# Chaining the two heads' weights-times-values products of a dense pair, key block by key block

## Chip, cores and metric

One NeuronCore of a Trainium2 chip runs the whole kernel. The metric is the device time of one execution in microseconds; the median of three runs of the kernel before is 1922.91 us (1922.61 to 1922.99). The granted TensorE clock was 0.997 of the full clock over the profiled execution.

## The reference, cut to what matters

The reference is a network of five mixing layers and one feed-forward layer over 512 tokens of width 1024. Three kinds of layer use dense causal softmax attention, which is where the change lies: the NSA layer (8 heads; its selected-block branch and its window branch both cover all earlier keys at this length), the MLA layer (twice, 16 heads) and the FOX layer (16 heads, with a forget term in the scores). The sliding-window layer has a code of its own. The dense part is

```
s = q @ k.T * scale            # 512 x 512 a head, keys after the query masked out
p = softmax(s)
o = p @ v                      # head width 64
```

## The kernel before, in words

All data is float32. Projections, scores and the output products are made of two- or three-term splits (`fp32r` tiles named `h` and `l`; lines 273 to 275, 309 and 310). The transposes of the softmax weights (line 335) and their products with the values (line 342) are plain float32 matmuls, and each of these float32 matmuls shows as two records of TensorE in the trace.

Heads are worked two at a time, a pair. For each head `dense_head` goes over the four blocks of 128 queries: scores into a PSUM tile `s`, mask and row maximum on VectorE (line 322), exponential on ScalarE (line 325), scaling by the reciprocal of the sum on VectorE (line 329), into an SBUF tile `sp`. Then it goes over the four blocks of 128 keys, j = 0 to 3: the 4 - j blocks of weights that see these keys are transposed on TensorE into a PSUM tile `t` (two buffers), and ScalarE copies the result into the SBUF tile `pt` (line 336, which calls the helper whose instruction is on line 205). So block j of `pt` has 512, 384, 256 or 128 columns.

`dense_values` then multiplies, for each key block j and each of the two heads i, the values of that block (128 keys x 64 channels, the stationary operand) with block j of the head's `pt`, and accumulates in one PSUM tile `o` (one buffer): head 0 in partitions 0 to 63, head 1 in partitions 64 to 127. That is 8 matmuls for each pair and branch. The FOX layer has 8 pairs, each MLA layer 8, and the NSA branch has 4 pairs with two branches each, 32 pairs in all. `gated` (line 950), or a copy, takes the pair's result out of `o`.

The program is written with a tile framework. Its scheduler orders the instructions of each engine once, when the kernel is built: a list scheduler with a timeline simulation that takes, for each engine, the earliest instruction in program order that is ready at that moment. It places the semaphores. So the order on an engine is not that of the source: the projections of the next heads, of gates (`gates`, `gate_tile`) and, in NSA, of `fill_gate` and `fill_up` are later in the program and are set into gaps. At run time each engine works through its fixed order.

In the three callers the two heads' `dense_head` come first and then `dense_values` (lines 790 to 792, 1059 to 1061, 1268 to 1270):

```
pt.append(self.dense_head(P, scores))
...
po = self.pso()
self.dense_values(po, pt, lambda jj, hh: ...)
```

The tile `pt` has two buffers in these stages, `sp` two (three in NSA).

Of the kernel before, what the change touches and what calls it, by code (L numbers as in the profile page):

```python
# [13 lines left out]
AF = mybir.ActivationFunctionType  # L14
# [6 lines left out]
NB = 4  # L21
# [28 lines left out]
TOFF = [0, 512, 896, 1152]  # L50
# [77 lines left out]
class Net:  # L128
# [73 lines left out]
            self.vcopy(out, in_, scale)  # L202

    def acopy(self, out, in_, scale=None):
        self.nc.scalar.activation(out, in_, AF.Copy, scale=1.0 if scale is None else scale)  # L205

    def vcopy(self, out, in_, scale=None):
        if scale is None:
# [103 lines left out]
    def dense_head(self, P, scores, gate=None, bufs=None):  # L312

        nc = self.nc
        sp = P.tile([128, 1280], F32, name="sp", bufs=bufs)
        mx, nm, sm, rc = (self.sm(NB, n) for n in ("mx", "nm", "sum", "rc"))
        for b in range(NB):
            n, g = (b + 1) * 128, slice(b, b + 1)
            v = sp[:, POFF[b]:POFF[b] + n]
            ps = self.pss()[:, 0:n]  # L320
            scores(ps, slice(b * 128, n), slice(0, n))
            nc.vector.tensor_tensor_reduce(  # L322
                out=v, in0=ps, in1=self.causal[:, S - n:S], scale=1.0, scalar=LOWEST, op0=ALU.add, op1=ALU.max, accum_out=mx[:, g])
            nc.vector.tensor_scalar(nm[:, g], mx[:, g], -1.0, None, ALU.mult)  # L324
            nc.scalar.activation(v, v, AF.Exp, bias=nm[:, g], accum_out=sm[:, g])  # L325
            nc.vector.reciprocal(rc[:, g], sm[:, g])
            if gate is not None:
                nc.vector.tensor_tensor(out=rc[:, g], in0=rc[:, g], in1=gate[:, g], op=ALU.mult)
            nc.vector.tensor_scalar(v, v, rc[:, g], None, ALU.mult)  # L329
        pt = P.tile([128, 1280], F32, name="pt")  # L330
        for j in range(NB):
            ps = self.pst()
            n = (NB - j) * 128
            for b in range(j, NB):
                nc.tensor.transpose(ps[:, (b - j) * 128:(b - j + 1) * 128], sp[:, POFF[b] + j * 128:POFF[b] + j * 128 + 128], self.ident)  # L335
            self.acopy(pt[:, TOFF[j]:TOFF[j] + n], ps[:, 0:n])
        return pt

    def dense_values(self, po, pts, value, first=True, last=True):
        for j in range(NB):  # L340
            for i, pt in enumerate(pts):
                self.nc.tensor.matmul(  # L342
                    po[64 * i:64 * i + 64, j * 128:S], lhsT=value(j, i), rhs=pt[:, TOFF[j]:TOFF[j] + (NB - j) * 128],
                    start=first and j == 0, stop=last and j == NB - 1, skip_group_check=not (first and last))


    def to_feat(self, src, b, scale=None, pool=None):
# [965 lines left out]
```

## Time and profile before

| what | value |
|---|---|
| median of three runs | 1922.91 us |
| the profiled execution | 1921.38 us |
| its span, first to last instruction | 1919.6 us |
| TensorE busy (matmul) | 1880.0 us, 98% |
| VectorE busy | 1153.4 us, 60% |
| ScalarE busy | 878.2 us, 46% |
| GpSimd busy | 156.4 us, 8% |
| mean load on 16 DMA engines | 77 GB/s |

The profile is of one execution. Busy time is the time in which an engine has at least one instruction open. The records of TensorE overlap, since a matmul is let in before the one ahead has drained, and their ends are modelled; the distance from one start to the next tells how long one matmul holds TensorE.

### The profile page before, as it was taken

The numbers are of one execution on the slowest core, as the hardware profiler recorded it, in microseconds if no ns is written. First come the engines' busy times: TensorE is split into PE (matmuls) and PEld (weight loads), VectorE is DVE, ScalarE is ACT, GpSimd is POOL, SyncE is SP. The second block draws the span as 40 slices with busy tenths as digits, with TensorE's granted clock in tenths as the row PEclk, the third lists the DMA queues.
The fourth block names the chain that finished last, engine by engine and source line by source line (L and its number), as shares of the span: only waits on it lengthen the run. The fifth ranks groups of instructions, "written<-read, shape, count | busy, mean of one in ns | idle before, by whom it ended". The sixth has DMA issues, their size and how long they took to land.

```text
span 1919.6 us, 26637 instructions
## 1 busy us (share of the span) xinstructions
PE 1880.0 (98%) x9843; PEld 1496.4 (78%) x9843; DVE 1153.4 (60%) x2954; ACT 878.2 (46%) x1970; POOL 156.4 (8%) x213
## 2 busy tenths in 40 slices
PE   8999899999999999999999999999999999999997
PEld 7777677678888888889777788877887777987775
DVE  5554486754533343256878675577765665787765
ACT  4543245642322132135666434563555563466651
POOL 2221200000000000001000011251000000200001
PEclk9999999999999999999999999999999999999999
DMA  7222041042422243133221133212422231231111
GB/s 212 78 55 67 4 133 50 17 133 87 122 88 82 75 129 99 60 95 96 56 62 55 56 100 91 67 53 60 110 66 55 67 96 49 76 88 49 58 45 44
DMA packets 200781, 148.09 MB, mean 77 GB/s; under 512 B 8797, under 2 KB 178570, under 8 KB 200650
## 3 DMA queue, kind: packets, MB, share of 16 engines
q1 hardware_dynamic: 198858, 140.97, 25.4%
q0 software_dynamic: 1792, 5.42, 0.9%
q8 instruction: 77, 1.26, 0.3%
q14 instruction: 54, 0.44, 0.1%
HBM read 144.27 MB, written 2.10 MB: 76 GB/s over the span
## 4 chain that ended last, share of the span: by engine, by line
PE 84%; DVE 2%; issue 1%; ACT 1%; POOL 0%; DMA 0%; POOLq 0%; DVEq 0%; ACTq 0%
PE pj L273 22%; PE pj L275 21%; PE pj L274 21%; PE o L342 6%; PE t L335 4%; PE s L273 1%; PE s L309 1%; PE s L274 1%; PE s L275 1%; PE s L310 1%; PE t L358 1%; PE t L1166 1%; PE s L1265 1%; PE s L1266 1%; PE o L1121 1%
## 5 line engine op out<-in xcount | busy, mean ns | idle before, releaser
L214 ACT ACTIVATE wh<-wr 128x1024 fp32r<-128x1024 f32 (+9 forms) x390 | 281.3, 749 | 459.5 <-PE pj L274 272.5
L215 DVE TENSOR_TENSOR wl<-wr,wh 128x1024 fp32r<-128x1024 f32 (+9 forms) x390 | 321.7, 847 | 229.2 <-ACT wh L214 226.6
L273 PE MATMUL pj<-Ah,wh 128*128 128x512 f32 (+1 forms) x1120 | 434.8, 389 | 1.3 <-DVE k4l L215 0.8
L274 PE MATMUL pj<-Al,wh 128*128 128x512 f32 (+1 forms) x1120 | 433.5, 387 | 0.0
L275 PE MATMUL pj<-Ah,wl 128*128 128x512 f32 (+1 forms) x1120 | 433.5, 388 | 0.0
L273 PEld LDWEIGHTS pj<-Ah,wh 128*128 128x128 f32 x1120 | 210.6, 188 | 47.6 <-issue 3.1
L275 PEld LDWEIGHTS pj<-Ah,wl 128*128 128x128 f32 x1120 | 210.8, 188 | 45.2 <-issue 2.2
L274 PEld LDWEIGHTS pj<-Al,wh 128*128 128x128 f32 x1120 | 210.8, 188 | 43.3 <-issue 1.6
L273 PE MATMUL pj<-wh,Ah 128*128 128x512 f32 (+5 forms) x640 | 218.5, 342 | 3.8 <-ACT Ah L214 3.8
L274 PE MATMUL pj<-wl,Ah 128*128 128x512 f32 (+5 forms) x640 | 216.5, 339 | 0.0
L275 PE MATMUL pj<-wh,Al 128*128 128x512 f32 (+5 forms) x640 | 214.6, 340 | 0.5 <-DVE Al L215 0.4
L325 ACT ACTIVATE sp<-sp,nm 128x128 f32<-128x128 f32 (+3 forms) x256 | 142.7, 558 | 95.6 <-DVE nm L324 93.6
L322 DVE CUSTOM_DVE_ANT_0 sp<-s,c_causal 128x128 f32<-128x128 f32 (+3 forms) x256 | 121.9, 487 | 90.7 <-PE s L275 38.7
L205 ACT ACTIVATE pt<-t 128x512 f32<-128x512 f32 (+3 forms) x288 | 119.5, 445 | 122.9 <-PE t L335 99.3
L273 PEld LDWEIGHTS pj<-wh,Ah 128*128 128x128 f32 x640 | 121.5, 190 | 19.3 <-ACT Ah L214 5.7
L275 PEld LDWEIGHTS pj<-wh,Al 128*128 128x128 f32 x640 | 121.0, 190 | 15.4 <-issue 2.4
L274 PEld LDWEIGHTS pj<-wl,Ah 128*128 128x128 f32 x640 | 121.6, 190 | 11.6 <-issue 1.1
L335 PE MATMUL t<-ident,sp 128*128 128x128 f32 x640 | 111.7, 279 | 2.4 <-ACT pt L205 2.3
L335 PEld LDWEIGHTS t<-ident,sp 128*128 128x128 f32 x640 | 76.6, 140 | 47.2 <-ACT pt L205 16.8
L329 DVE TENSOR_SCALAR sp<-sp,rc 128x128 f32<-128x128 f32 (+3 forms) x256 | 96.7, 383 | 4.5
L342 PE MATMUL o<-pt,vt 128*64 128x512 f32 (+3 forms) x384 | 92.2, 452 | 0.0
L274 PE MATMUL pj<-wl,hdh 128*128 128x512 f32 x176 | 68.3, 390 | 0.0
(417 smaller groups left out, 2853.7 us busy)
## 6 DMA issues: line engine op xcount, KB each, us to landing
wr<-in_w_in_dram SPq DMA_DIRECT2D x34, 512.0 KB, 3.8
wr<-in_fox_w_in_dram SPq DMA_DIRECT2D x30, 512.0 KB, 4.2
wr<-in_w_ffn_gate_dram SPq DMA_DIRECT2D x22, 512.0 KB, 3.9
wr<-in_w_ffn_up_dram SPq DMA_DIRECT2D x22, 512.0 KB, 4.1
wr<-in_w_ffn_down_dram SPq DMA_DIRECT2D x20, 512.0 KB, 3.6
wr<-in_swa_w_in_dram SPq DMA_DIRECT2D x20, 512.0 KB, 4.4
wr<-in_mla_w_in_dram SPq DMA_DIRECT2D x16, 512.0 KB, 4.4
wr<-in_mla_w_out_dram SPq DMA_DIRECT2D x16, 512.0 KB, 3.8
```

What stands on the lines that cost most here:

```text
L205: self.nc.scalar.activation(out, in_, AF.Copy, scale=1.0 if scale is None else scale)
L214: self.nc.scalar.activation(h, src, AF.Copy)
L215: self.nc.vector.tensor_tensor(out=l, in0=src, in1=h.bitcast(F32), op=ALU.subtract)
L273: self.nc.tensor.matmul(ps, lhsT=ah, rhs=bh, start=i == 0, stop=False)
L274: self.nc.tensor.matmul(ps, lhsT=ah, rhs=bl, start=False, stop=False)
L275: self.nc.tensor.matmul(ps, lhsT=al, rhs=bh, start=False, stop=i == n - 1)
L309: self.nc.tensor.matmul(ps, lhsT=q, rhs=kh, start=True, stop=False)
L322: nc.vector.tensor_tensor_reduce(out=v, in0=ps, in1=self.causal[:, S - n:S], scale=1.0, scalar=LOWEST, op0=ALU.add, op1=ALU.max, accum_out ...
L325: nc.scalar.activation(v, v, AF.Exp, bias=nm[:, g], accum_out=sm[:, g])
L329: nc.vector.tensor_scalar(v, v, rc[:, g], None, ALU.mult)
L335: nc.tensor.transpose(ps[:, (b - j) * 128:(b - j + 1) * 128], sp[:, POFF[b] + j * 128:POFF[b] + j * 128 + 128], self.ident)
L342: self.nc.tensor.matmul(po[64 * i:64 * i + 64, j * 128:S], lhsT=value(j, i), rhs=pt[:, TOFF[j]:TOFF[j] + (NB - j) * 128], start=first and ...
```

## The change

`acopy` returns its instruction, `dense_head` returns its `pt` together with the last of its four copies, and a new helper `after` records a dependency between two instructions. In `dense_values` the heads are taken in the order 1, 0 for each key block. The first of the eight matmuls gets a real dependency (with a wait) on the last copy of both heads; each further matmul is only told to stand behind the one before it on the same engine, which needs no semaphore.

```diff
     def acopy(self, out, in_, scale=None):
-        self.nc.scalar.activation(out, in_, AF.Copy, scale=1.0 if scale is None else scale)
+        return self.nc.scalar.activation(out, in_, AF.Copy, scale=1.0 if scale is None else scale)
...
-            self.acopy(pt[:, TOFF[j]:TOFF[j] + n], ps[:, 0:n])
-        return pt
+            turned = self.acopy(pt[:, TOFF[j]:TOFF[j] + n], ps[:, 0:n])
+        return pt, turned.ins
+
+    def after(self, later, earlier, how=mybir.DependencyClass.NoSync):
+        self.tc.add_manual_dep(later, earlier.name, mybir.DependencyInfo(how, mybir.DependencyReason.DATA), reason="order")
 
     def dense_values(self, po, pts, value, first=True, last=True):
+
+        prev = None
         for j in range(NB):
-            for i, pt in enumerate(pts):
-                self.nc.tensor.matmul(
+            for i in (1, 0):
+                pt, turned = pts[i]
+                mm = self.nc.tensor.matmul(
                     po[64 * i:64 * i + 64, j * 128:S], lhsT=value(j, i), rhs=pt[:, TOFF[j]:TOFF[j] + (NB - j) * 128],
-                    start=first and j == 0, stop=last and j == NB - 1, skip_group_check=not (first and last))
+                    start=first and j == 0, stop=last and j == NB - 1, skip_group_check=not (first and last)).ins
+                if prev is None:
+                    for _, t in pts:
+                        self.after(mm, t, mybir.DependencyClass.Sync)
+                else:
+                    self.after(mm, prev)
+                prev = mm
```

## Rows read from the trace of the kernel before

**Rows 1.** The page: span, and TensorE's busy time, share and instructions.
```profile
span 1919.6 us, 26637 instructions
...
PE 1880.0 (98%) x9843; PEld 1496.4 (78%) x9843; DVE 1153.4 (60%) x2954; ACT 878.2 (46%) x1970; POOL 156.4 (8%) x213
```
**Rows 2.** Windows of a stage: from:to, length, busy us (count) of each engine, clock, DMA.
```profile
915.00:1085.00 170.00, 169.62 (x879) 125.42 (x878) 128.76 (x432) 104.33 (x280) 1.14 (x2) 1.00 0.19 59
...
380.00:390.00 10.00, 10.00 (x56) 6.79 (x56) 8.41 (x49) 7.30 (x23) 0.00 (x0) 1.00 0.17 53
```
**Rows 3.** Line 342 alone: its window; its first and last visit in TensorE's timeline.
```profile
0.00:1920.00 1920.00, 123.35 (x512) 38.26 (x512) 1.00 0.27 77
...
286.32 1.07 PE L342 MATMUL o<-pt,X 128*64 128x512 f32 x2
...
1878.69 1.51 PE L342 MATMUL o<-pt,vt 128*64 128x384 f32 x10
```
**Rows 4.** TensorE's timeline, one MLA pair: start us, busy us, line, operation, count.
```profile
933.51 0.49 PE L335 MATMUL t<-ident,sp 128*128 128x128 f32 x3
933.93 1.07 PE L342 MATMUL o<-pt,vt 128*64 128x512 f32 x2
934.93 0.33 PE L273 MATMUL s<-k4h,qh 128*128 128x128 f32 x1
...
941.91 1.07 PE L342 MATMUL o<-pt,vt 128*64 128x512 f32 x4
...
943.30 0.86 PE L342 MATMUL o<-pt,vt 128*64 128x384 f32 x4
...
946.73 0.65 PE L342 MATMUL o<-pt,vt 128*64 128x256 f32 x4
...
947.78 0.43 PE L342 MATMUL o<-pt,vt 128*64 128x128 f32 x2
```
**Rows 5.** TensorE's timeline, a later pair: longer visits, seven transposes, the score after.
```profile
966.59 1.72 PE L342 MATMUL o<-pt,vt 128*64 128x512 f32 x8
...
971.22 0.86 PE L342 MATMUL o<-pt,vt 128*64 128x256 f32 x6
972.02 0.98 PE L335 MATMUL t<-ident,sp 128*128 128x128 f32 x7
972.76 0.42 PE L273 MATMUL s<-k4h,qh 128*128 128x384 f32 x1
```
**Rows 6.** TensorE's timeline, sliding-window layer: first record of a visit, the instruction after it.
```profile
1204.10 0.54 PE L1121 MATMUL o<-pt,vt 128*64 128x128 f32 x5
...
1205.77 0.33 PE L309 MATMUL s<-k0h,q 128*128 128x128 f32 x1
```
**Rows 7.** Timelines: two pairs' last copies on ScalarE, the second's last visit on TensorE.
```profile
966.59 0.55 ACT L205 ACTIVATE pt<-t 128x256 f32<-128x256 f32 x2 [1.03 <-PE t L335]
...
1818.77 0.28 ACT L205 ACTIVATE pt<-t 128x128 f32<-128x128 f32 x1 [0.46 <-PE t L335]
...
1820.25 0.43 PE L342 MATMUL o<-pt,vt 128*64 128x128 f32 x2
```
**Rows 8.** End of the first MLA layer, TensorE and ScalarE; TensorE's waits over the kernel.
```profile
1088.40 0.44 PE L335 MATMUL t<-ident,sp 128*128 128x128 f32 x2 [0.64 <-ACT pt L205]
...
1090.04 1.51 PE L342 MATMUL o<-pt,vt 128*64 128x384 f32 x10
1092.27 0.50 PE L273 MATMUL pj<-wh,Ah 128*128 128x512 f32 x1 [0.72 <-ACT Ah L214]
...
1087.75 0.98 ACT L205 ACTIVATE pt<-t 128x512 f32<-128x512 f32 x2 [2.53 <-PE t L335]
1088.88 0.38 ACT L205 ACTIVATE pt<-t 128x256 f32<-128x256 f32 x1
1090.14 0.28 ACT L205 ACTIVATE pt<-t 128x128 f32<-128x128 f32 x1 [0.88 <-PE t L335]
...
PE t L335 <- ACT pt L205: 2.3, 5, 0.6
```

## Prediction, before the changed kernel was run

> **What bounds the kernel now.** I began with the page. TensorE is busy for 98% of a span of 1919.6 us [rows 1], so the question is whether the edit takes TensorE time away, and whether what remains can still be fed. The busy figure is modelled with overlap, so I then took windows of the stages that call the edited function. In the first MLA layer (915 to 1085 us) TensorE is busy 169.6 of 170 us, VectorE 128.8 and ScalarE 104.3; in a dense stretch of the NSA branch VectorE is busy 8.4 of 10 us [rows 2]. The granted clock is 1.00, the 2.4 GHz level, in both. TensorE is the bound there, VectorE the next.
>
> Next I asked for the edited line alone: 512 matmul records, 123.35 us busy [rows 3]. Each of the 256 matmuls in the source (32 pairs of heads, 8 each) leaves two records. In the timeline these records stand in visits, runs with no other TensorE work between; I counted 126, and rows 3 show the first and the last. A visit's busy time runs about 0.07 us past the start of the next instruction (933.93 + 1.07 against 934.93, [rows 4]); all lengths below are busy times less 0.07. So the 126 visits hold TensorE for 123.35 - 126 x 0.07 = 114.5 us, 3.58 us a pair.
>
> Rows 4 show one pair from start to end, five visits spread over 14 us with other work between. The first, a lone 512-column matmul (two records), lasts 1.00 us. The second has four records, a 512-column matmul of head 1 and a 384-column one of head 0, and also lasts 1.00 us. So a matmul that writes partitions 64 to 127 runs beside one that writes 0 to 63 and adds nothing. The next lasts 0.79 (384 beside 256), the next 0.58 (256 beside 128), and a lone 128-column one follows (0.36). Head 0 runs one key block ahead, so its first and head 1's last matmul have no partner.
>
> A visit costs something by itself too. Seven transposes take 0.74 us from 972.02 to 972.76, 0.106 each [rows 5]; the three before the visit at 933.93 take 0.42, which is 0.10 more than 3 x 0.106 [rows 4]. I count 0.10 us for each entry. The drain at the end lies in the visit's own time.
>
> **The change, part by part.** The return values and the helper issue nothing. No operand, size or instruction count changes, and no DMA is added or moved by the edit itself. What changes is when the eight matmuls of a pair may start (the first now waits for the last ScalarE copy of both heads) and their order (head 1 then head 0, block by block).
>
> *Pairing and merging.* After the first wait nothing within the eight waits for anything new, so I take one visit a pair. Its length comes from longer visits that exist. Eight records, 384 beside 256 behind 512 beside 384, last 1.65 us instead of 1.00, so a 384-led step adds 0.65 [rows 4, 5]. Ten records, led by 384, 256 and 128 columns, last 1.44 us (1.51 - 0.07, the last of rows 3) instead of 0.79, so the 256- and 128-led steps together add 0.65. Six, led by 256 and 128, last 0.79 instead of 0.58, so 0.21 of that is the 128-led step and 0.44 the other. As a partner is free, 512, 384, 256 and 128 columns with equal partners take 1.00 + 0.65 + 0.44 + 0.21 = 2.30 us. Equal partners do not occur on this line, but they do in the sliding-window layer: 26 records of 128 columns, 13 matmuls, run from 1204.10 to 1205.77 [rows 6]. That is seven steps of 0.21 and 0.2 us at the end, not thirteen steps (2.7 us). The gain is 32 x (3.58 - 2.30) = 41.0 us.
>
> One rule of the Trainium skill speaks against free partners: the page "TensorE: Matmul & The Clock Gate", section "Measured speedup vs the span model", gives 2.38 times, not 3, for three column tiles. By that, as an estimate, two tiles would give 2 x 2.38 / 3 = 1.59 times, a pair's 4.4 us of single steps would take 2.8 and 0.1 at the end, 0.6 more than my 2.30, and the 41.0 us would be some 22. The trace disagrees so far: 1.00 us with a partner and without.
>
> *Entries.* 126 - 32 = 94 entries at 0.10 are 9.4 us. Pairing and entries together are 50.4 us, the upper bound of the gain. The lower bound of the entries is nothing, if other work is still set between the matmuls.
>
> *The new wait.* Behind the waiting matmul on TensorE's queue stands everything that follows in the fixed order; VectorE's gating of the pair waits for the last of the eight. What hides the wait is how early the copies are: in the pair at 966 us the last copies of head 1 begin at 966.59 and end at 967.14, and the visit that needs them starts at 971.22, 4.1 us later [rows 5, 7]. I compared every pair: in 28 of 32 the last copy ends before the last visit starts, at the least 1.2 us before (1818.77 + 0.28 against 1820.25). Gathering all eight at that place costs nothing where other matmuls fill TensorE in the meantime, as the projections do.
>
> In four pairs, the last of the NSA branch and of each MLA and FOX layer, that cover is gone. There the last visit of the first MLA layer starts at 1090.04 while the last copy starts only at 1090.14, and TensorE idles 0.64 us for a copy and 0.72 us afterwards [rows 8]. At present the values are what fills the copies' time. After the change, four copies back to back from 1087.75 take 0.98 + 0.38 + 0.28 = 1.64 us, to 1089.4; with 0.2 us until TensorE starts and 2.30 us of matmuls the pair ends at 1091.9, against 1090.04 + 1.51 = 1091.55 now. So the tail gets 0.35 us longer, while 1.10 us of the lone first visit leaves its earlier place: a gain of about 0.7 instead of 1.57, or 4 x 0.9 = 3.6 us less in all.
>
> *Everything else.* VectorE and ScalarE do the same work in less time: MLA would go from 170 to some 157 us, with VectorE at 82%. The whole order is set anew, and I can't cost that from the trace; from below it is nothing, from above the half of the gain (rivals). I take a tenth, 4.7 us, near the lower end, because in the whole kernel TensorE's transposes waited for these copies 2.3 us in five places [rows 8].
>
> *Sum.* 50.4 - 3.6 - 4.7 = 42.1 us. The profiled execution took 1921.4 us (span 1919.6), which gives 1879.3; the median of the runs shown is 1.5 above, so I say **1880 us**.
>
> **Rivals.**
> - *Split visits.* The chain fixes an order, not adjacency. If every key block's two heads run together but other work stands between blocks, a pair needs 1.00 + 0.79 + 0.58 + 0.36 = 2.73 and four entries, 3.13, against 3.58 + 126/32 x 0.10 = 3.97 now: 27 us gained, 1894. For it speaks that fillers now stand between visits; against it, that ready matmuls already merge to eight and ten records.
> - *The chain behind TensorE becomes the bound.* VectorE stands at 8.4 of 10 us in NSA; if a pair takes some 14 us, as the one of rows 4, then 1.57 us less, 11%, would bring it to 9.4. If half of the gain becomes waits for VectorE or ScalarE, about 23 us remain: 1898. Against it: MLA and FOX have more room, and projections can be drawn forward.
> - *Partners slow each other.* If equal partners share something that unequal ones don't, a step is at worst 1.67 / 7 = 0.24 us instead of 0.21, should nothing of the sliding-window visit be its end [rows 6]. A seventh more on 2.30 us is 0.33 a pair, 11 us: 1891. Against it, the drain at the end of every visit explains the difference. By the page's figure above it would be 0.6 us a pair, and the time 1898.
> - *The wait shows (slower).* It decides if, at the place where the eight stand, the next transposes and both heads' copies have no other TensorE work beside them, as at the layer ends. The bubble is then about 1.64 us of copies plus the 0.2 us to start, 1.84, which is 0.27 more than the gain of 1.57 a pair; over 32 pairs 9 us slower, 1930. The break-even is a bubble of 1.57 us in every pair. Against it stand the 4 us of rows 5 and 7.
> - *No overlap in the new order (slower).* Were the two heads not run side by side, a pair would take at least 2 x (0.90 + 0.65 + 0.44 + 0.21) + 0.1 = 4.5 us plus one entry, 4.6 against 3.97 (0.90 is the lone 1.00 without some 0.1 for the drain at its end): 20 us slower, 1941. Rows 4 and 6 all but exclude it.
> - *Nothing changes*, if the order already written were what is emitted. It isn't: head 0's first block runs alone in all 32 pairs.
>
> **How the numbers follow.** My forecast has 0.60 (own range 1868 to 1892), split visits 0.12, the bound moved 0.11, slowed partners 0.04, the wait 0.09, no overlap 0.02, no change 0.02. A difference below 0.2% (3.8 us) can't be told from none here. Faster is 0.60 + 0.12 + 0.11 + 0.04 = 0.87, slower 0.11, same 0.02. The range reaches from 1868, the full 50.4 us with a few more for a luckier order, to 1910, which takes in the three weaker gains and leaves out the slower cases and the edges.
>
> **What would show it.** Right: 32 visits of 16 records, each 2.3 us to the next start; busy time of the line near 32 x 2.37 = 76 us; ScalarE's copies ending before the visit except at four layer ends, where TensorE's idle time ahead of the visit grows by about 1 us; VectorE's busy time unchanged in a shorter span. Wrong: more than 32 visits (split), visits longer than 2.4 us (partners), waits of TensorE for VectorE between transposes and scores (bound moved), or for the copies in most pairs (the wait).

## The result, and the profile after

The changed kernel takes 1879.19 us (median of five runs, 1878.14 to 1880.77) against 1922.91 us before: a ratio of 0.9774, 95% interval 0.9763 to 0.9785, or 43.7 us less. The profiled execution took 1878.37 us, 43.0 less than that of before.

The page of the changed kernel, span and TensorE:

```profile
span 1876.6 us, 26623 instructions
...
PE 1830.0 (98%) x9843; PEld 1491.2 (79%) x9843; DVE 1149.9 (61%) x2954; ACT 873.6 (47%) x1970; POOL 156.7 (8%) x213
```

Against [rows 1], TensorE has lost 50.0 us of busy time with the same 9843 matmuls. VectorE and ScalarE do the work they did. The span shrinks by 43.0 us, so TensorE idles 7 us more.

The edited line alone (now line 348), as a window over the whole span:

```profile
0.00:1880.00 1880.00, 75.97 (x512) 33.93 (x512) 1.00 0.27 79
```

123.35 us of [rows 3] became 75.97, with the same 512 records. TensorE's timeline shows why, here an MLA pair and the end of the first MLA layer:

```profile
936.99 0.34 PE L274 MATMUL s<-k4l,qh 128*128 128x384 f32 x1
937.16 0.27 PE L335 MATMUL t<-ident,sp 128*128 128x128 f32 x1
937.36 2.37 PE L348 MATMUL o<-pt,vt 128*64 128x512 f32 x16
939.67 0.87 PE L335 MATMUL t<-ident,sp 128*128 128x128 f32 x6
...
1066.29 0.65 PE L335 MATMUL t<-ident,sp 128*128 128x128 f32 x4
1067.52 0.71 PE L335 MATMUL t<-ident,sp 128*128 128x128 f32 x3 [0.58 <-ACT pt L205]
1068.60 2.37 PE L348 MATMUL o<-pt,vt 128*64 128x512 f32 x16 [0.37 <-ACT pt L205]
1071.71 0.50 PE L273 MATMUL pj<-wh,Ah 128*128 128x512 f32 x1 [0.74 <-ACT Ah L214]
```

All sixteen records of a pair are one visit (a run of the line's records with no other TensorE work between), 937.36 to 939.67, 2.31 us, where [rows 4] had five visits. There are 32 such visits in the trace, one for each pair; 28 take 2.30 to 2.31 us to the next start, and in the four at the ends of the NSA branch and of the layers an idle time of 0.7 us stands behind.

ScalarE's timeline at the same places, the last copies of that pair and the four of the layer's last head:

```profile
932.77 0.53 ACT L205 ACTIVATE pt<-t 128x256 f32<-128x256 f32 x2
...
1066.87 1.68 ACT L205 ACTIVATE pt<-t 128x512 f32<-128x512 f32 x4 [1.14 <-PE t L335]
```

In the first pair the last copy ends at 933.30, 4.1 us before the visit. At the layer's end it ends at 1068.55 and the visit starts 0.05 us later: there the wait is on the path. The waits of TensorE over the whole kernel:

```profile
PE t L335 <- ACT pt L205: 4.8, 13, 0.6
...
PE o L348 <- ACT pt L205: 1.7, 5, 0.4
```

Transposes wait for these copies 4.8 us instead of the 2.3 of [rows 8]; the visits themselves waited in five places. Four are the predicted ends; the fifth lies in the NSA branch.

The first matmul after the NSA branch and after each of the three dense layers dates the stages. Before:

```profile
400.49 0.73 PE L273 MATMUL pj<-kw1h,wh 128*128 128x512 f32 x2 [0.69 <-ACT kw1h L214]
...
1612.78 0.50 PE L273 MATMUL pj<-wh,Ah 128*128 128x512 f32 x1 [0.72 <-ACT Ah L214]
...
1880.92 0.50 PE L273 MATMUL pj<-wh,Ah 128*128 128x512 f32 x1 [0.72 <-ACT Ah L214]
```

After:

```profile
391.41 0.50 PE L273 MATMUL pj<-kw1h,wh 128*128 128x512 f32 x1 [0.70 <-ACT kw1h L214]
...
1581.01 0.50 PE L273 MATMUL pj<-wh,Ah 128*128 128x512 f32 x1 [0.73 <-ACT Ah L214]
...
1837.92 0.50 PE L273 MATMUL pj<-wh,Ah 128*128 128x512 f32 x1 [0.74 <-ACT Ah L214]
```

With 1092.27 of [rows 8] and 1071.71 above, the lead grows to 9.1 us at the end of NSA, 20.6 at the end of the first MLA layer, 31.8 after FOX and 43.0 after the second MLA layer: 9.1, 11.5, 11.2 and 11.2 us a stage. Between these stages nothing beyond 0.1 us is gained or lost. Ahead of the first one little is: line 784 (now 796), the first matmul of NSA's dense part, starts at 279.64 us before and at 279.79 after, so that part alone gained 9.2 us.

### The profile page after: what moved, and what is told of

The parts are those of the page before. It is cut to its first block, busy times and chain, and to the rows that moved or that the text cites. A ratio compares the mean times of both kernels' runs of the same rounds, so it can differ in the third digit from the quotient of the medians.

```text
span 1876.6 us, 26623 instructions
## 1 busy us (share of the span) xinstructions
PE 1830.0 (98%) x9843; PEld 1491.2 (79%) x9843; DVE 1149.9 (61%) x2954; ACT 873.6 (47%) x1970; POOL 156.7 (8%) x213
## 4 chain that ended last, share of the span: by engine, by line
PE 81%; DVE 3%; ACT 2%; issue 1%; POOL 0%; DMA 0%; POOLq 0%; DVEq 0%; ACTq 0%
PE pj L273 22%; PE pj L274 22%; PE pj L275 22%; PE o L348 4%; PE t L335 3%; PE s L309 1%; PE s L274 1%; PE s L273 1%; PE s L275 1%; PE s L310 1%; PE t L370 1%; ACT pt L205 1%; PE t L1178 1%; PE s L1278 1%; PE s L1277 1%
## 5 line engine op out<-in xcount | busy, mean ns | idle before, releaser
L274 PE MATMUL pj<-wl,Ah 128*128 128x512 f32 (+5 forms) x640 | 215.9, 338 | 0.0
L205 ACT ACTIVATE pt<-t 128x512 f32<-128x512 f32 (+3 forms) x288 | 114.9, 445 | 114.4 <-PE t L335 74.8
L335 PE MATMUL t<-ident,sp 128*128 128x128 f32 x640 | 107.9, 277 | 4.9 <-ACT pt L205 4.8
L335 PEld LDWEIGHTS t<-ident,sp 128*128 128x128 f32 x640 | 77.3, 140 | 30.4 <-ACT pt L205 11.5
L275 PE MATMUL pj<-wh,hdl 128*128 128x512 f32 x176 | 68.3, 389 | 0.0
```

What stands on the lines that cost most here:

```text
L205: return self.nc.scalar.activation(out, in_, AF.Copy, scale=1.0 if scale is None else scale)
L274: self.nc.tensor.matmul(ps, lhsT=ah, rhs=bl, start=False, stop=False)
L275: self.nc.tensor.matmul(ps, lhsT=al, rhs=bh, start=False, stop=i == n - 1)
```

## The experiments

The theory: a pair costs TensorE its passes, with the partner's free, and some 0.1 us for each entry into a visit and 0.1 for the drain at its end; the wait costs only where no other TensorE work covers it. The rivals: gathering alone pays; the chain or the order of the heads matters; entries are hidden. Every kernel was timed beside the kernel before, and the ratios are to that kernel; each profile shows one execution.

**Head by head.**
```diff
-        for j in range(NB):
-            for i in (1, 0):
+        for i in (1, 0):
+            for j in range(NB):
```


> The wait and the chain stay, but all four matmuls of head 1 come before the four of head 0, so each pair is still one visit without partners. Main theory (running the two heads side by side is most of the gain): a visit takes 2 x (0.90 + 0.65 + 0.44 + 0.21) + 0.1 = 4.5 us instead of 2.30, 32 x 2.2 = 70 us more than the changed kernel, 1945 to 1955 us, slower than the kernel before. Rival (gathering a pair into one visit is what pays, or TensorE pulls the second head forward by itself): visits stay near 2.3 us and the time near 1879.

1928.02 us, ratio 1.0029 (1.0017 to 1.0041). The line's window:

```profile
0.00:1930.00 1930.00, 125.69 (x512) 57.90 (x512) 1.00 0.26 77
```

32 visits again, of 125.69 / 32 - 0.07 = 3.86 us. The span is 49.9 us longer than that of the changed kernel, and 32 x (3.86 - 2.30) is 49.9. Against before, the longer visits cost 32 x (3.86 - 3.58) = 9.0 us, about what 94 entries fewer save (9.4), and the kernel is 5.3 us slower than the kernel before timed beside it (1922.71). So gathering that gives up most partners is worth nothing: the rival falls. The step of my expectation that failed is "no partners": 3.86, not 4.5. The starts of the records in one visit show it (columns, us from the visit's start):

```
512 0.00, 512 0.48, 384 0.91, 384 1.23, 256 1.55, [512 1.56], 256 1.77, 128 1.99, [512 2.04], 128 2.10, [384 2.47] ...
```

The bracketed records are the second head's. Its first starts beside the first head's third block, ahead of three records written before it. All 32 visits show this order of starts.

**The chain without the wait.**
```diff
-                if prev is None:
-                    for _, t in pts:
-                        self.after(mm, t, mybir.DependencyClass.Sync)
-                else:
+                if prev is not None:
                     self.after(mm, prev)
```


> The chain and the order stay, the wait for both heads' last copies goes: a key block's two matmuls can run as soon as their own copies are done. Main theory: partners stay together (a few may be parted), the eight split into some 90 visits, each additional one costs about 0.10 us of entry and 0.10 us of drain at its end, 58 x 0.2 = 12 us, of which the shorter layer ends give back 4 x 0.35 us: 1887 to 1892 us. Rival (entries and drains are hidden, and the wait for the last copies is what costs in the NSA branch and at layer ends): 1873 to 1877, faster than the changed kernel.

1889.56 us, ratio 0.9825 (0.9809 to 0.9841): 10.4 us slower than the changed kernel. The line's window:

```profile
0.00:1890.00 1890.00, 91.32 (x512) 29.51 (x512) 1.00 0.27 78
```

There are 90 visits, which hold TensorE for 91.32 - 90 x 0.07 = 85.0 us against 75.97 - 32 x 0.07 = 73.7. That is 11.3 us for 58 more visits, in the visits themselves. It is not 0.10 each: where a visit splits between key blocks the parts are 0.15 longer together (1.01 + 0.80 against 1.65 for the 512- and the 384-column step), 8 us for 55 splits, and in three pairs the two 512-column matmuls were parted, 1.0 each. Entries at 0.10 would add 5.8. Of these 17 us the kernel shows 10.4 (13.1 between the profiled spans); the rest came back, since TensorE's transposes waited 3.1 us for copies in 8 places and the visits not at all. So the chain without the wait, which pairs nearly all matmuls and gathers a part (126 visits become 90), gives about 33 of the 44 us, and the wait's gathering the rest.

**The wait without the chain, and the other order.** The first makes all eight matmuls wait and drops the chain, the second turns `(1, 0)` into `(0, 1)`.

> All eight matmuls of a pair wait for both last copies, no chain among them; written order as in the change. Main theory: all eight become ready at one moment, the scheduler takes them in program order, so the visits stay whole: 1877 to 1881 us. Rival (the chain is what keeps the eight together): visits split, 1887 us or more.

> As the change, but head 0 before head 1 in each key block. Main theory: only that neighbours belong to different heads matters; 32 visits of 2.30 us, 1876 to 1883 us. Rival (head 1 must go first, since its matmul is the one that starts the accumulation on the upper partitions or its data comes last): visits longer than 2.4 us and at least 4 us slower than the changed kernel.

1879.54 us, ratio 0.9773 (0.9758 to 0.9788), and 1878.91 us, 0.9771 (0.9757 to 0.9786). Both have 32 whole visits, and the first has the same order of instructions on TensorE as the changed kernel. So the wait is enough by itself: once all eight are ready at the same moment the scheduler takes them in program order. Beside the wait, neither the chain nor head 1 in front adds anything that can be measured.

**By twos.** After the head-by-head run, an order between the two:
```diff
-        for j in range(NB):
-            for i in (1, 0):
+        for j0 in (0, 2):
+            for i, j in ((1, j0), (1, j0 + 1), (0, j0), (0, j0 + 1)):
```


> As the change, but ordered by twos: head 1's blocks 0 and 1, head 0's 0 and 1, head 1's 2 and 3, head 0's 2 and 3. The head-by-head order showed TensorE starting a matmul of the other head four records ahead of its turn, not five. Theory (a look-ahead of about four records): here the other head's first record is four ahead at the start, so nearly all runs side by side: visits of 2.3 to 2.6 us, 1879 to 1890 us. Rival (only the neighbouring matmul is started early, and the head-by-head overlap has another cause): visits of 3.0 us or more, 1900 us or more.

One run, 1878.99 us. The line's window:

```profile
0.00:1880.00 1880.00, 77.58 (x512) 39.17 (x512) 1.00 0.27 79
```

77.58 / 32 - 0.07 = 2.35 us a visit. The second head's first record starts 0.014 us behind the first head's, though three records stand between them in program order. All 32 visits do this (0.013 or 0.014 us). Side by side does not need neighbours in program order.

**Where the NSA branch falls short.** Its dense part gained 9.2 us, the other stages 11.2 to 11.5. TensorE's waits in its dense part, before (250 to 400.4 us):

```profile
PE s L309 <- DVE mx L322: 1.2, 2, 0.6
PE t L335 <- ACT pt L205: 0.3, 1, 0.3
```

and after (250 to 391.4):

```profile
PE t L335 <- ACT pt L205: 1.9, 6, 0.5
PE s L309 <- DVE mx L322: 1.3, 3, 0.6
PE o L348 <- ACT pt L205: 0.6, 2, 0.4
```

1.5 us became 3.8, mostly for ScalarE's copies. ScalarE in turn waits for the values to release a `pt`, which it did nowhere in the branch before: 4.4 us in three places (300 to 392 us), at one of them 2.52 us:

```profile
ACT pt L205 <- PE o L348: 4.4, 3, 2.5
...
384.35 1.68 ACT L205 ACTIVATE pt<-t 128x512 f32<-128x512 f32 x4 [2.52 <-PE o L348]
```

So a third `pt` was tried, with `sp` giving up its third buffer, hence a control. The diff shows the line of each of the two runs; the other uses of `sp` and `pt` in the branch get the same numbers of buffers.
```diff
-                        pts.append(self.dense_head(..., gate=gv, bufs=3))
+                        pts.append(self.dense_head(..., gate=gv))            # control: sp 2, pt 2
+                        pts.append(self.dense_head(..., gate=gv, ptb=3))     # sp 2, pt 3
```


> Control for the next run: as the change, but two buffers instead of three for the scores sp of the NSA branch. No theory of the change speaks of it: 1879 to 1890 us.

> As the control, with three buffers instead of two for the turned weights pt of the NSA branch. Theory A (the NSA branch falls some 2.5 us short since ScalarE's copies of the next head wait for a pt that the gathered matmuls release late): 1.5 to 3 us faster than the control. Theory B (the shortfall comes from the copies' own chain of two PSUM tiles t and from VectorE, and a third pt only moves the wait): within 1 us of the control.

1886.17 us, 0.9812 (0.9798 to 0.9827), and 1885.63 us, 0.9810 (0.9793 to 0.9826). A third `pt` gives nothing with two `sp`. But this does not test theory A: in the control ScalarE waits nowhere in the branch for the values to release a `pt`, so the wait that a third one was to remove is already gone. Another has come, VectorE's for transposes to release an `sp` (0.8 us in the changed kernel, 0.4 before):

```profile
DVE sp L322 <- PE t L335: 6.4, 6, 4.8
```

Whether a third `pt` helps with three `sp` stays open. The 8.2 us that the control lost by the branch's end are not all waits either: behind them TensorE's clock fell (the changed kernel shows 1.00 there), and the last visit took 4.45 us instead of 2.37. The run with the third `pt` has the same fall (4.47 us). The windows of the control, with the granted clock third from the end:

```profile
392.00:396.00 4.00, 3.10 (x9) 1.27 (x11) 0.00 (x0) 1.53 (x4) 0.00 (x0) 0.50 0.00 0
396.00:400.00 4.00, 3.30 (x16) 1.51 (x13) 0.39 (x1) 0.60 (x1) 0.42 (x1) 0.66 0.01 1
```

**No wait at the ends.**
```diff
-                    for _, t in pts:
+                    for _, t in pts if gather else ():
...
+        gather=pr < 3                       # NSA
+        gather=quad * 2 + pr < KD - 1       # MLA, FOX
```


> As the change, but without the wait for the last copies where little other TensorE work is left: the last pair of each MLA and FOX layer and the last two (one pair of heads, two branches) of the NSA branch. Main theory (there the wait itself is on the path): the stretch from the first copy of the last head to the next layer's first matmul goes from 4.84 back to some 4.5 us, 0.3 us in each of three layers, and the NSA branch gets back 1 to 2 of the 4 us by which it falls short of its 12.8: 1875 to 1878 us. Rival (the additional visits, 0.2 us each, eat what the earlier start gives, and the NSA branch is short for other reasons): within 1 us of the changed kernel, or slower.

1876.85 us, ratio 0.9768 (0.9755 to 0.9782). The end of the first MLA layer, TensorE and ScalarE:

```profile
1067.17 1.08 PE L348 MATMUL o<-pt,vt 128*64 128x512 f32 x4
1068.18 0.33 PE L335 MATMUL t<-ident,sp 128*128 128x128 f32 x1
1068.44 1.52 PE L348 MATMUL o<-pt,vt 128*64 128x384 f32 x12
1070.69 0.50 PE L273 MATMUL pj<-wh,Ah 128*128 128x512 f32 x1 [0.73 <-ACT Ah L214]
...
1066.16 1.51 ACT L205 ACTIVATE pt<-t 128x512 f32<-128x512 f32 x3 [1.14 <-PE t L335]
```

From the first of the last head's copies to the next matmul it takes 4.53 us, against 1071.71 - 1066.87 = 4.84 with the wait and 1092.27 - 1087.75 = 4.52 before [rows 8]. So the wait lengthens a layer's end by 0.31 us. NSA's dense part, from its first matmul to the first one after it, takes 110.65 us instead of 111.62, 1.0 less, at the low end of what was expected. The gain in time, some 2 us, lies within the intervals of the timed runs, but the profiles of this run and of the two combined ones below agree on it stage by stage (110.64 to 110.67 us in NSA, 4.54 at the end of each MLA and FOX layer, against 111.62 and 4.84 in the changed kernel): 1.0 and three times 0.3 us.

**The same wait in the sliding-window layer.** All 14 matmuls of a pair there wait for both heads' last copies.
```diff
+                            for mm in mms:
+                                for _, turned in pt:
+                                    self.after(mm.ins, turned, mybir.DependencyClass.Sync)
```


> As the change, and the sliding-window layer's 14 matmuls of a pair also wait for the last copies of both heads (no chain). Main theory (a pair costs its passes, half of them free beside a partner, and about 0.10 us an entry and a drain a visit): its 21 visits become 8. Eight lone matmuls go (0.36 + 0.10 us each, 3.7 us) and five parted pairs join (1.02 + 1.02 + 0.10 - 1.67, 0.47 us each, 2.4 us); 6.0 us less work, of which waits at that layer's end may take 1 to 2: 1873 to 1876 us. Rival (the layer is held by VectorE and GpSimd between heads, so TensorE only waits longer): within 2 us of the changed kernel.

1877.01 us, ratio 0.9766 (0.9752 to 0.9781). Its 21 visits became 8 of 1.73 us, which takes 4.3 us out of the visits, besides 13 entries. But in the layer TensorE now waits longer for VectorE's masking of scores (the changed kernel, then this run):

```profile
PE s L309 <- DVE mx L1155: 1.0, 3, 0.4
...
PE s L309 <- DVE mx L1158: 4.5, 8, 1.3
```

3.5 of the 6.0 us expected go there. The stretch from the end of the first MLA layer to that of the sliding-window layer is 2.0 us shorter in the profile (213.9 us against 215.9); the timed runs can't tell the kernel from the changed one.

**Both together, and once more without the sliding-window layer's last pair.**

> The sliding-window waits of the earlier run and the missing waits at the ends together. Main theory: the two add up, 2 us from the one and 1 to 3 from the other: 1873 to 1876 us. Rival: the ends give nothing, 1877 us.

> As the run before with the sliding-window waits and the ends, but the sliding-window layer's last pair doesn't wait either. In the run before, TensorE's clock fell to 0.50 near that layer's end, behind 0.95, 0.19 and 0.41 us of idle time. Theory (the waits give their gain wherever other work covers them and cost at every layer end): no fall of the clock there, and the parts add up, 1873 to 1875.5 us, 2 to 5 us faster than the changed kernel in the same call. Rival (the order that the scheduler finds scatters by 2 us whatever one does): 1876 to 1878 us.

> The changed kernel itself, as the control of the run beside it: 1878 to 1881 us.

1876.61 us (0.9771, 0.9758 to 0.9785), 1877.93 us (0.9770, 0.9756 to 0.9784) and, for the changed kernel beside the latter, 1878.49 us (0.9770, 0.9756 to 0.9784). The parts don't add up, and the theory that they would by sparing every end is not borne out. The profiles tell which part is missing: the ends give their 1.9 us in both, but the stretch with the sliding-window layer takes 216.1 and 216.4 us instead of 213.9. In both, TensorE's clock stood at its 1.2 GHz level for some 3.4 us there, in the first run from 1279.8 us, in the second from 1217.2; the run with the sliding-window waits alone shows 1.00 at both places. At half the clock that is at most 1.7 us (an estimate), the larger part of the 2.2 and 2.5 that are missing. No version is faster than the changed kernel by more than the timed runs can tell.

## Why the prediction was right

It said 1880 us from 42.1 us of gain; 1879.2 and 43.0 us between the profiled executions were measured. The mechanism it named is what the trace shows; that the sum comes within a microsecond also owes something to luck, since 4.7 us of it was a choice. Term by term:

- **Pairing and merging, 41.0 us.** Measured: 114.5 - 73.7 = 40.8 us. The visit put together from longer ones was 2.30 us, and is. That a partner of equal size is free is shown: 512 beside 512 columns fits the same sum that unequal partners gave.
- **Entries, 9.4 us.** There are 94 fewer. The run without the wait agrees in size: its span is 13.1 us longer though its waits for copies are 3.4 us shorter (3.1 against 4.8 + 1.7), 16.5 us more work, of which 11.3 lie in the visits; the 5.2 left are 0.09 for each of 58 entries, if nothing else changed. So 0.10 remains an estimate, not isolated.
- **The layer ends, 3.6 us.** The longer tail was put at 0.35 us each and is 0.32 (4.84 against 4.52), and the run without the wait there removes it. The four copies take 1.68 us back to back (1.64 predicted), and TensorE starts 0.05 us after them, not 0.2. The sign named for it was too large: TensorE's idle time for these copies grew by 0.3 us (0.64 to 0.58 + 0.37), not by about 1.
- **The tenth, 4.7 us, that nothing accounted for.** Of 40.8 + 9.4 = 50.2 us the kernel kept 43.0; 7.2 are gone, against 3.6 + 4.7 = 8.3 predicted. The 4.7 had no source but a choice near the lower end, and it wasn't spread evenly: MLA and FOX kept 11.2 to 11.5 us of the 12.6 - 0.9 = 11.7 predicted for eight pairs (before the tenth), while NSA's dense part kept 9.2. Of the 2.5 missing there, 2.3 are TensorE's longer waits, and the wait showed at one pair more than predicted. This is the one place where the cover was judged too well: I had read it from MLA pairs, with 4 us between copy and visit, but in NSA projections hold TensorE for 47 of 110 us (98 of 160 in MLA), and for only 2.3 of the last 20. The trace points at the `pt` buffers: a gathered visit keeps both until its end, and ScalarE's copies for the next pair wait for them, which they did not before. Without the wait at the branch's end (the run above) the longest of these waits fell from 2.52 to 1.86 us and the part got 1.0 us shorter, but no run isolates the buffers.
- **Rivals.** Split visits is what the chain alone gives (90 visits, 1890 us; 1894 was worked out for a fourfold split). Written head by head, the case of no overlap, the kernel is 5.3 us slower than before and not the 20 worked out, since TensorE finds some partners by itself. Slower partners are excluded by 2.30 us. The bound did not move in MLA, where TensorE is busy 168.0 and VectorE 135 of 170 us:

```profile
893.00:1063.00 170.00, 168.00 (x935) 134.63 (x934) 135.27 (x443) 109.64 (x288) 1.13 (x2) 1.00 0.20 60
```

## What to carry to other kernels

When TensorE is the bound, look at how matmuls that fill only half of its columns stand in the timeline: one whose neighbours write the other half is nearly free, and one alone pays in full. A list scheduler that starts each matmul when its own data is ready pulls such partners apart; making them wait for their common last input puts them back, at no cost as long as other matmuls fill the time, and at a small price where nothing does: here 0.3 us at the end of a layer and 1.0 in the NSA branch. The price of a layout can be read from the trace of before by taking a few longer visits apart.

## What the hardware showed unexpectedly

**TensorE looks ahead.** In the order by twos, the other half's matmul started 14 ns behind the first with three records that the program has ahead of it not yet started; in the head-by-head order it didn't start with four such records waiting, and did with three. The Trainium skill, page "TensorE: Matmul & The Clock Gate", section "The mechanism", says that matmuls start and end in strict program order; these two runs disagree. What sets the reach of three records was not tried further.

**The clock fell behind an idle stretch in one run and not in another.** In the last sliding-window run, granted clock and work around 1217 us (windows, then TensorE's timeline):

```profile
1212.00:1216.00 4.00, 3.31 (x17) 2.51 (x15) 1.73 (x5) 1.65 (x2) 0.79 (x1) 1.00 0.00 0
1216.00:1220.00 4.00, 3.06 (x8) 2.37 (x9) 3.25 (x13) 2.16 (x9) 1.64 (x2) 0.65 0.36 131
...
1216.72 0.38 PE L309 MATMUL s<-k1h,q 128*128 128x256 f32 x1 [1.11 <-DVE mx L1158]
...
1217.44 0.79 PE L273 MATMUL pj<-Ah,wh 128*128 128x512 f32 x1 [0.22 <-DVE q L297]
1218.03 0.63 PE L274 MATMUL pj<-Al,wh 128*128 128x512 f32 x1
...
1221.31 0.40 PE L274 MATMUL pj<-Al,wh 128*128 128x512 f32 x1
```

Behind waits of 1.11 and 0.22 us the clock goes to its 1.2 GHz level, and the projections show 0.63 us busy instead of 0.40 until 2.4 GHz returns. In the run with the sliding-window waits alone, waits of 1.12 and 0.22 us stand at the same place, and the clock stays at 1.00:

```profile
1216.00:1220.00 4.00, 3.11 (x13) 2.46 (x14) 3.20 (x13) 2.16 (x9) 1.63 (x2) 1.00 0.46 131
```

So idle time can cost more than its own length. With one profile of each kernel, what decides between the two outcomes stays open.
